# Two-block transformer kernel: S5 parameters in whole rows, x and the first weights in turns on one queue, loads moved from ACT's queue

## The chip, the cores and the metric

The kernel runs on one core of a Trainium2 chip. The metric is the device time of one execution in microseconds. The engines are TensorE (PE in the rows, PEld its weight loads), VectorE (DVE), ScalarE (ACT), GpSimd (POOL) and SyncE (SP); a q behind a name (ACTq) is that engine's instruction queue when it issues a DMA.

## The reference

256 tokens of width 2048 pass two layers of a first block and one layer of a second. Everything is float32. Cut to what matters:

```python
def layer_even(x, norm_g, w_in, w_out):          # first layer
    h = rmsnorm(x, norm_g)
    qa, ka, va, iq, ik, iw, qb, kb, vb, gate = split_cols(h @ w_in, SPLIT0)
    ... # attention A on the 64 best keys by an index score (iq, ik, iw); attention B with dilated windows
    return x + (concat(o_a, o_b) * silu(gate)) @ w_out

def s5_branch(u, z, a_re, a_im, log_dt, b_re, b_im, c_re, c_im, ...):   # in the second block
    dt = exp(log_dt)[:, None]
    mag = exp(a_re * dt)
    ab_re, ab_im = mag * cos(a_im * dt), mag * sin(a_im * dt)
    ...                                          # bb from ab, a and b; a scan over the tokens; c reads it out
```

The state-space parameters are small: a_re and a_im are 64 groups x 64 states, log_dt is one number a group, b_re and b_im are 64 x 64 x 16, c_re and c_im 64 x 16 x 64.

## The kernel before

A projection (`projW`, line 178) multiplies the normed input by a group of weight columns. float32 accuracy comes from three matmuls in a faster format: input and weights are each split into a high and a low part (`split`, line 145: ACT casts the high part at line 147, DVE subtracts to get the low part at lines 106 and 150), and high x high, high x low and low x high are summed in PSUM. Weights come in chunks of 256 rows (`weights`, line 157): one DMA on SP's queue for each run of columns at line 170 (six `raw` buffers), one cast, one subtraction (three buffers `wh` and `wl`), then 24 matmuls for four blocks of 128 columns. The chunk loads and splits stand at a raised priority. The code is traced in program order, and a scheduler puts each engine's instructions into an order by priority and by its own model of when each is ready; at run time an engine takes them in that order, its DMA issues among them, and waits for each.

`first_block` (line 613) starts the work. norm0's rows and the four pieces of x (256 tokens x 512 columns, 512 KB) are loaded from ACT's queue (lines 1507 and 626). `feed` (line 247) turns a piece on TensorE (line 127, eight transposes a piece) and splits it with norm0 as a factor (ACT line 118, DVE line 109). `squares`, `rstd` and `bcast` make the row norm's inverse: ACT squares, DVE sums, POOL takes the power (line 142), TensorE and ACT spread it over the partitions as `rb`. `params` (line 1517) then loads 15 rows of parameters from ACT's queue and turns them (lines 1507, 1511, 1513, 1541).

`even_layer` (line 387) projects in this order: a small group (ka, va, ik, iw: 336 columns, two DMAs a chunk), two groups of iq, three groups of qa. Each projection's PSUM (two buffers) is emptied at once by `rope` on DVE, scaled by rb; `ev_small` also turns iw and va on TensorE within its evacuation (lines 417 to 422). Behind the last qa group, at `K.hook()` (line 431), `s5_params` (line 670) is traced: nine loads from ACT's queue in the layout in which they are used (128 partitions = two groups x 64 states), so that a_re, a_im and log_dt are read 4 bytes at a time and b_re and b_im 64 bytes at a time (lines 683 to 688); then a chain of small operations on DVE and ACT in two scratch tiles (`yh`, `yl`), and sixteen transposes. Its results go to DRAM for later. After it come the attention `att()` (index scores, top-k on DVE, softmax), which runs beside the further projections, and the gate projections, which wait for it.

Of the kernel before, what the change touches and what calls it, by code (L numbers as in the profile page):

```python
# [16 lines left out]
D = 2048  # L17
S = 256
# [7 lines left out]
LAT = dict(bc=8.5, fd=10.0, fb=1.2, fh=0.8, z=0.3, sm=8.85, pt=1.42, st=6.0, ix=0.55, top=9.0, s5=11.0, inv=32.0, pr=1.3,  # L26
# [26 lines left out]
class Ker:  # L53
    def __init__(self, tc, a, es):
        self.tc, self.nc, self.a, self.es = tc, tc.nc, a, es
        self.n = 0
        self.after = lambda: None
# [62 lines left out]
    def mm(self, out, l, r, st=True, sp=True, **k):  # L120
        n = int(np.prod(r.shape[1:])) / 2.4
        self.clock += n if r.dtype == F32R else 4 * n * l.shape[0] / 128
        return self.nc.tensor.matmul(out, l, r, start=st, stop=sp, **k)  # L123
# [21 lines left out]
    def split(self, h, l, src, scale=None):  # L145
        if scale is None:
            self.nc.scalar.copy(h, src)  # L147
            self.tt(l, src, h.bitcast(F32), ALU.subtract)
        else:
            self.act(h, src, AF.Copy, scale=scale)  # L150
            self.stt(l, src, scale, h.bitcast(F32), ALU.mult, ALU.subtract)
# [5 lines left out]
    def weights(self, w, blocks, nk=KT, pool=None):  # L157
        runs, off = [], 0
        for c0, n in [r for b in blocks for r in (b if isinstance(b, list) else [b])]:
            if runs and runs[-1][0] + runs[-1][1] == c0:  # L160
                runs[-1][1] += n
            else:
                runs.append([c0, n, off])
            off += n
        KC = self.KC
        for kc in range(0, nk, KC):
          with self.tc.high_priority(offset=self.HP):
# [79 lines left out]
    def feed(self, xg, g, x, nw, ss=None):  # L247
        if ss is not None:
            self.squares(xg, g, ss)
        for k2 in range(0, 4, 2):  # L250
            pt = self.ps().rearrange("p (k s) -> p k s", k=2)
            for k in range(2):
                for t in range(2):
                    self.tr(pt[:, k, t * 128:t * 128 + 128], xg[:, t, (k2 + k) * 128:(k2 + k) * 128 + 128])
            for k in range(2):
                kk = 4 * g + k2 + k
                self.split(x[0][:, kk], x[1][:, kk], pt[:, k], nw if isinstance(nw, float) else nw[:, kk:kk + 1])

    def rstd(self, ss, name, n=D):
# [3 lines left out]
        r = self.t(self.pc, [128, 2], name)  # L263
# [4 lines left out]
    def bcast(self, r, name):  # L268
        o = self.t(self.pc, [128, S], name)
# [117 lines left out]
def even_layer(K, x, rbc, r, yo):  # L387
    nc, a = K.nc, K.a
    with ExitStack() as es:
# [19 lines left out]

        def ev_small(pt):  # L410
            K.tt(rp, rp, rbc.unsqueeze(1).to_broadcast([128, 4, S]), ALU.mult)
# [4 lines left out]
            K.tt(iwz[0:16], pt[64:80, 2], rbc[64:80], ALU.mult)  # L416
            p = K.ps()
# [12 lines left out]

        K.hook()
# [181 lines left out]
def first_block(K):  # L613
# [5 lines left out]
    with ExitStack() as es:  # L619
        K.pwk = K.pool("pre", 2, es)  # L620
        with K.tc.high_priority(offset=20000):
            n0 = load_params(K, [("norm0", a["norm0"].rearrange("(b p) -> b p", p=128), 16)], "pn", K.pwk)["norm0"]
            xgs = []
            for g in range(4):
                xg = K.t(K.pwk, [128, 2, 512], "xg", bufs=4)
                nc.scalar.dma_start(xg, xin[:, g * 512:g * 512 + 512].rearrange("(t p) c -> p t c", p=128))
                K.feed(xg, g, xt, n0)
                xgs.append(xg)
        for g in range(4):
            K.squares(xgs[g], g, ss[0])  # L630
        r0 = K.rstd(ss[0], "r0")
        rb0 = K.bcast(r0, "rb")
    prm = params(K)
# [3 lines left out]
    T = {}  # L637

# [31 lines left out]
def s5_params(K, ha, hb):  # L670
# [4 lines left out]
    dma = nc.scalar.dma_start  # L675
# [824 lines left out]
def load_params(K, rows, name, pool):  # L1500

    nc = K.nc
    t = K.t(pool, [128, 128], "prow")
    o = 0
    where = {}
    for key, ap, n in rows:
        nc.scalar.dma_start(t[o:o + n], ap)
        where[key] = (o, n)
        o += n
# [12 lines left out]
def params_(K, pool):  # L1522
# [5 lines left out]
                          ("kk", rw(a["rwkv_k_k_2"][0]), 8), ("ka", rw(a["rwkv_k_a_2"][0]), 8)], "pa", pool)  # L1528
# [3 lines left out]
                               ("gnw", a["gdn_norm_w_2"], 1)], "pb", pool))  # L1532
    prm.update(load_params(K, [("conv", a["gdn_conv_w_2"][0].rearrange("j (b p) -> (j b) p", p=128), 96)], "pv", pool))
# [247 lines left out]
```

## Time and profile before

| | us |
|---|---|
| median of 3 runs | 2217.39 (2214.86 to 2219.24) |
| the profiled execution, its own time | 2214.52 |
| its span, first to last instruction | 2212.7 |
| TensorE busy (matmul) | 2136.3, 97% |
| DVE busy | 1624.6, 73% |
| ACT busy | 1000.8, 45% |
| POOL busy | 37.8, 2% |

Busy shares are means over the whole span. The slices and windows of the rows below give them by stage. A matmul's duration overlaps the next one's, so the pace of matmuls is read from their count in a window; the granted clock beside it is 1.00 at 2.4 GHz and 0.50 at 1.2 GHz.

### The profile page before, as it was taken

Reading aid. Unit: us, or ns where it says so; the run is one execution under the profiler, and the core shown is the slowest. Engines: PE = TensorE matmul, PEld = TensorE weight load, DVE = VectorE, ACT = ScalarE, POOL = GpSimd, SP = SyncE. Lnnn points to the kernel's source line nnn. Section 1 sums busy time; section 2 is a strip of 40 time slices with the busy share of each in tenths; the row PEclk is TensorE's granted clock in tenths of the full one; section 3 lists DMA queues with packets and bytes.
Section 4 is the critical chain, followed back from the end, with each engine's and each line's share of the span. In section 5 each row is a group of like instructions: output and inputs, shape, how many; then the busy total and the mean of one; then the engine's idle time right before and its main releaser. Section 6 shows DMA issues by size and latency. Waiting matters only on the chain.

```text
span 2212.7 us, 38063 instructions
## 1 busy us (share of the span) xinstructions
PE 2136.3 (97%) x14946; PEld 1943.4 (88%) x14946; DVE 1624.6 (73%) x2845; ACT 1000.8 (45%) x1421; POOL 37.8 (2%) x85
## 2 busy tenths in 40 slices
PE   7499999999999999999999999999999999999998
PEld 7399999989989999989999989977778978979886
DVE  4387866657799866665578988989898857765665
ACT  4134454454345344454544433434346545534443
POOL 0010000000000000000000000000000000000000
PEclk9699999999999999999999999999999999999999
DMA  7355665676766665667677675676756667685774
GB/s 211 77 172 183 184 183 154 207 230 202 223 193 183 200 201 153 228 223 237 195 197 211 192 205 179 189 231 198 224 172 213 190 194 238 198 282 155 268 239 152
DMA packets 304249, 440.44 MB, mean 199 GB/s; under 512 B 73541, under 2 KB 135238, under 8 KB 303814
## 3 DMA queue, kind: packets, MB, share of 16 engines
q1 hardware_dynamic: 252048, 428.70, 62.7%
q10 hardware_dynamic: 52022, 9.31, 2.3%
q8 instruction: 117, 1.92, 0.4%
q14 instruction: 62, 0.51, 0.1%
HBM read 396.37 MB, written 41.57 MB: 198 GB/s over the span
## 4 chain that ended last, share of the span: by engine, by line
PE 81%; DVE 9%; DMA 4%; ACTq 2%; issue 2%; ACT 1%; POOL 0%; SPq 0%; DVEq 0%; POOLq 0%
PE pj L123 70%; PE ps L123 9%; DVE wl L106 3%; PE ps L127 2%; ACTq L687 1%; DMA raw<-in_w_in_dram 1%; DVE s5w L106 1%; DMA dim<-b 1%; DVE b L106 1%; ACTq L688 1%; ACT wh L147 1%; DMA e<-dim 1%; DMA s5r<-s5u 0%; POOL grs L142 0%; DVE G L106 0%
## 5 line engine op out<-in xcount | busy, mean ns | idle before, releaser
L147 ACT CAST wh<-raw 128x1024 fp32r<-128x1024 f32 (+5 forms) x680 | 685.0, 1009 | 950.9 <-PE pj L123 757.4
L106 DVE TENSOR_TENSOR wl<-raw,wh 128x1024 fp32r<-128x1024 f32 (+5 forms) x680 | 794.9, 1171 | 410.5 <-ACT wh L147 398.7
L123 PE MATMUL pj<-xh,wh 128*128 128x256 f32 (+1 forms) x2864 | 825.2, 288 | 13.9 <-ACT wh L147 13.0
L123 PE MATMUL pj<-xh,wl 128*128 128x256 f32 (+1 forms) x2864 | 816.1, 285 | 1.3 <-DVE wl L106 1.2
L123 PE MATMUL pj<-xl,wh 128*128 128x256 f32 (+1 forms) x2864 | 814.6, 284 | 0.3 <-DVE xl L109 0.3
L123 PEld LDWEIGHTS pj<-xh,wh 128*128 128x128 f32 (+1 forms) x2864 | 550.8, 192 | 26.7 <-ACT wh L147 13.4
L123 PEld LDWEIGHTS pj<-xh,wl 128*128 128x128 f32 (+1 forms) x2864 | 550.6, 192 | 6.0 <-issue 2.8
L123 PEld LDWEIGHTS pj<-xl,wh 128*128 128x128 f32 (+1 forms) x2864 | 551.0, 192 | 1.7 <-DVE xl L109 0.6
L123 PE MATMUL pj<-wh,xh 128*128 128x512 f32 (+2 forms) x736 | 283.4, 385 | 0.0
L123 PE MATMUL pj<-wh,xl 128*128 128x512 f32 (+2 forms) x736 | 279.1, 379 | 0.0
L123 PE MATMUL pj<-wl,xh 128*128 128x512 f32 (+2 forms) x736 | 278.8, 379 | 0.0
L123 PEld LDWEIGHTS pj<-wh,xh 128*128 128x128 f32 x736 | 138.8, 189 | 24.5 <-issue 3.0
L123 PEld LDWEIGHTS pj<-wl,xh 128*128 128x128 f32 x736 | 138.8, 189 | 23.6 <-issue 1.6
L123 PEld LDWEIGHTS pj<-wh,xl 128*128 128x128 f32 x736 | 138.6, 188 | 23.8 <-issue 1.2
L123 PE MATMUL pj<-wl,yh 128*128 128x512 f32 x256 | 99.9, 390 | 0.0
L123 PE MATMUL pj<-wh,yl 128*128 128x512 f32 x256 | 99.9, 390 | 0.0
L123 PE MATMUL pj<-wh,yh 128*128 128x512 f32 x256 | 99.7, 389 | 0.0
L123 PE MATMUL pj<-wh,E 128*128 128x512 f32 x192 | 76.7, 399 | 0.5 <-ACT wh L147 0.5
L123 PE MATMUL pj<-wl,E 128*128 128x512 f32 x192 | 75.0, 391 | 0.8 <-DVE wl L106 0.8
L123 PE MATMUL pj<-wh,G 128*128 128x512 f32 x192 | 75.2, 391 | 0.0
L106 DVE TENSOR_TENSOR raw<-yh,yl 128x256 f32<-128x256 f32 (+7 forms) x256 | 63.9, 287 | 3.5
L123 PEld LDWEIGHTS pj<-wh,yl 128*128 128x128 f32 x256 | 48.1, 188 | 9.9
(409 smaller groups left out, 2107.8 us busy)
## 6 DMA issues: line engine op xcount, KB each, us to landing
raw<-in_w_in_dram SPq DMA_DIRECT2D x416, 512.0 KB, 4.1
raw<-in_w_out_dram SPq DMA_DIRECT2D x96, 512.0 KB, 5.0
raw<-in_w_in_dram SPq DMA_DIRECT2D x96, 256.0 KB, 3.0
raw<-in_w_branch_dram SPq DMA_DIRECT2D x48, 512.0 KB, 5.3
raw<-in_w_in_dram SPq DMA_DIRECT2D x24, 344.0 KB, 3.1
s5t<-yh SPq DMA_DIRECT2D x16, 512.0 KB, 6.6
s5tb<-s5t SPq DMA_DIRECT2D x32, 256.0 KB, 4.6
raw<-in_w_in_dram SPq DMA_DIRECT2D x16, 384.0 KB, 4.0
```

What stands on the lines that cost most here:

```text
L106: return (eng or self.nc.vector).tensor_tensor(out=out, in0=a, in1=b, op=op)
L123: return self.nc.tensor.matmul(out, l, r, start=st, stop=sp, **k)
L127: return self.nc.tensor.transpose(out, a, self.ident)
L147: self.nc.scalar.copy(h, src)
L687: dma(br, a["s5_b_re_2"][0].rearrange("(i j) p c -> (j p) i c", j=2))
L688: dma(bi, a["s5_b_im_2"][0].rearrange("(i j) p c -> (j p) i c", j=2))
```

## The change

- The a and b parameters of S5 are loaded with groups on the partitions, in whole rows (32 rows of two groups each). log_dt is copied along its rows by POOL. One transpose (of 96 rows) and sixteen (of 64) on TensorE turn them into the former layout; they are ordered behind the last matmul traced before the hook (`issue_after`). All loads and stores of `s5_params` go from ACT's queue to POOL's.
- The other parameter rows (`params`) are loaded from POOL's queue, norm0's from SP's.
- The x pieces are loaded from SP's queue, into a tile that the S5 scratch takes over later. A callback in `weights` (`ahead`) puts x piece g ahead of weight chunk 4g of the first projection, and `issue_after` pins loads and splits to the order x0, w0, w2, x1, w4, w6, x2 and so on. A piece's transposes may start behind the chunk before last; its squares stand between two chunks' splits.
- The first projection is now the first group of iq (four blocks, 512 columns), the small group comes second, and the turns of iw and va become a step of their own (`turn_small`), due 12 us after the small group.
- The warm-up activation goes to the front of ACT, eight extra matmuls on the identity to the front of TensorE and eight on the first x piece behind its transposes; no one reads their results.

The diff's core:

```diff
-        warm = self.t(self.pc, [128, 1], "warm")
-        self.act(warm, self.mhalf[:, 0:1], AF.Tanh)
+        with self.tc.high_priority(offset=40000):
+            warm = self.t(self.pc, [128, 1], "warm")
+            self.act(warm, self.mhalf[:, 0:1], AF.Tanh)
+            self.dummies(self.ident, 8)
+
+
+    def dummies(self, m, n):
+        p = self.t(self.pm[1], [128, 512], "ps1")
+        for _ in range(n):
+            self.nc.tensor.matmul(p[:, 0:128], self.ident, m, start=True, stop=True)
...
+    def linked(self):
+        es = ExitStack()
+        for i in self.order:
+            es.enter_context(self.tc.issue_after(i))
+        return es
...
+          self.ahead(kc)
+          with self.tc.high_priority(offset=self.HP), self.linked():
             raw = self.t(self.pw, [128, KC, off], "raw", bufs=6)
             for c0, n, o in runs:
-                self.nc.sync.dma_start(
+                d = self.nc.sync.dma_start(
                     raw[:, :, o:o + n],
                     w[kc * 128:(kc + KC) * 128, c0:c0 + n].rearrange("(k p) c -> p k c", p=128))
             h, l = (self.t(pool or self.pw, [128, KC, off], tag, F32R, bufs=8 if pool else 3) for tag in ("wh", "wl"))
-            self.split(h, l, raw)
+            i = self.split(h, l, raw)
+          if self.order:
+              self.order = [d.ins] + i
           yield kc, h, l
...
+        def ev_iq(pt, g):
+            if g == 0:
+                K.tt(rp, rp, rbc.unsqueeze(1).to_broadcast([128, 4, S]), ALU.mult)
+            K.rope(iq[:, 4 * g:4 * g + 4], pt, 4, 64, C2, T2)
+
...
+        def turn_small():
+            yield LAT["small"]
             p = K.ps()
             for t in range(2):
                 K.mm(p[:, t * 16:t * 16 + 16], iwz[:, t * 128:t * 128 + 128], K.ident[:, 0:16])
                 K.tr(p[:, 256 + t * 128:384 + t * 128], vaT[:, t * 128:t * 128 + 128])
             nc.vector.tensor_copy(iw, p[:, 0:32].rearrange("p (t c) -> p t c", t=2))
             nc.scalar.copy(va, p[:, 256:512].rearrange("p (t c) -> p t c", t=2))
+        qi = lambda g: K.projW(w, [(1536 + g * 512 + b * 128, 128) for b in range(4)], x, lambda pt: ev_iq(pt, g))
+        qi(0)
         K.projW(w, [(1280, 128), (1408, 128), (2560, 80)], x, ev_small)
-        for g in range(2):
-            K.projW(w, [(1536 + g * 512 + b * 128, 128) for b in range(4)], x,
-                    lambda pt, g=g: K.rope(iq[:, 4 * g:4 * g + 4], pt, 4, 64, C2, T2))
+        turned = K.flow(turn_small(), (0, 0, 0, 1))
+        qi(1)
...
-    with ExitStack() as es:
-        K.pwk = K.pool("pre", 2, es)
-        with K.tc.high_priority(offset=20000):
-            n0 = load_params(K, [("norm0", a["norm0"].rearrange("(b p) -> b p", p=128), 16)], "pn", K.pwk)["norm0"]
-            xgs = []
-            for g in range(4):
-                xg = K.t(K.pwk, [128, 2, 512], "xg", bufs=4)
-                nc.scalar.dma_start(xg, xin[:, g * 512:g * 512 + 512].rearrange("(t p) c -> p t c", p=128))
-                K.feed(xg, g, xt, n0)
-                xgs.append(xg)
-        for g in range(4):
-            K.squares(xgs[g], g, ss[0])
-        r0 = K.rstd(ss[0], "r0")
-        rb0 = K.bcast(r0, "rb")
-    prm = params(K)
     ey = ExitStack()
     py = K.pool("y0", 1, ey)
     spare = lambda p: [K.t(p, [128, 4096], t) for t in ("yh", "yl")]
     T = {}
+    xall, scr = spare(py)
+    xgs = [xall[:, 1024 * g:1024 * g + 1024].rearrange("p (t c) -> p t c", t=2) for g in range(4)]
+    with K.tc.high_priority(offset=20000):
+        n0 = load_params(K, [("norm0", a["norm0"].rearrange("(b p) -> b p", p=128), 16)], "pn", None, nc.sync.dma_start,
+                         scr[:, 0:128], K.order)["norm0"]
+    r0, rb0 = K.t(K.pc, [128, 2], "r0"), K.t(K.pc, [128, S], "rb")
+
+    prm, behind = {}, K.order[-1]
+
+
+
+    def ahead(kc):
+        nonlocal behind
+        g = kc // 4
+        if kc % 4 == 0:
+            with K.tc.high_priority(offset=20000), K.linked(), K.tc.issue_after(behind):
+                d = nc.sync.dma_start(xgs[g], xin[:, g * 512:g * 512 + 512].rearrange("(t p) c -> p t c", p=128))
+                i = K.feed(xgs[g], g, xt, n0)
+                if g == 0:
+                    K.dummies(xgs[0][:, 0, 0:128], 8)
+            K.order = [d.ins] + i
+            return
+        behind = K.last
+        with K.linked():
+            for t in range(2):
+                K.act(scr[:, 512 + 512 * t:1024 + 512 * t], xgs[g][:, t], AF.Square, accum_out=ss[0][:, t, g:g + 1])
+        if g == 3:
+            K.ahead, K.order = lambda kc: None, []
+            K.rstd(ss[0], "r0", r=r0)
+            K.bcast(r0, "rb", rb0)
+            prm.update(params(K))
+    K.ahead = ahead
...
-    dma = nc.scalar.dma_start
+    dma = nc.gpsimd.dma_start
     big = [ha[:, 512 * i:512 * i + 512] for i in range(8)]
     v32 = lambda x: x.rearrange("p (i c) -> p i c", c=16)
     br, bi, t2, bbr, bbi = (v32(x) for x in big[0:5])
@@ -680,12 +729,29 @@
     small = [big[7][:, 32 * i:32 * i + 32] for i in range(16)]
     take = lambda: small.pop(0)
     ar, ai, ld = take(), take(), take()
-    dma(ar, a["s5_a_re_2"][0].rearrange("(i j) p -> (j p) i", j=2))
-    dma(ai, a["s5_a_im_2"][0].rearrange("(i j) p -> (j p) i", j=2))
-    for j in range(2):
-        dma(ld[64 * j:64 * j + 64], a["s5_log_dt_2"][0].rearrange("(i j) -> j i", j=2)[j].partition_broadcast(64))
-    dma(br, a["s5_b_re_2"][0].rearrange("(i j) p c -> (j p) i c", j=2))
-    dma(bi, a["s5_b_im_2"][0].rearrange("(i j) p c -> (j p) i c", j=2))
+    Z, lj = big[3][0:96, 0:128], big[4][64:96, 0:2]
+    jp = lambda name: a[name][0].rearrange("(i j) p -> i (j p)", j=2)
+    dma(Z[0:32], jp("s5_a_re_2"))
+    dma(Z[32:64], jp("s5_a_im_2"))
+    dma(lj, a["s5_log_dt_2"][0].rearrange("(i j) -> i j", j=2))
+    B = hb[0:64, 2048:4096]
+    for i, name in enumerate(("s5_b_re_2", "s5_b_im_2")):
+        dma(B[32 * i:32 * i + 32], a[name][0].rearrange("(i j) p c -> i (j p c)", j=2))
+    nc.gpsimd.tensor_copy(Z[64:96].rearrange("i (j p) -> i j p", j=2), lj.unsqueeze(2).to_broadcast([32, 2, 64]))
+    behind = K.last
+    p = K.ps()
+    with K.tc.issue_after(behind):
+        nc.tensor.transpose(p[:, 0:96], Z, K.ident[0:96, 0:96])
+    nc.vector.tensor_copy(big[7][:, 0:96], p[:, 0:96])
+    Bc = B.rearrange("i (m c) -> i m c", c=16)
+    for c in (0, 8):
+        p = K.ps()
+        with K.tc.issue_after(behind):
+            for u in range(8):
+                nc.tensor.transpose(p[:, 64 * u:64 * u + 64], Bc[:, :, c + u], K.ident[0:64, 0:64])
+        pv = p.rearrange("p (c r i) -> p c r i", c=8, r=2)
+        for r, o in enumerate((br, bi)):
+            nc.scalar.copy(o[:, :, c:c + 8].rearrange("p i c -> p c i"), pv[:, :, r])
...
```

`load_params` takes the issuing queue as an argument: SP's for norm0, POOL's in the three calls of `params`. `rstd` and `bcast` can take a ready tile, and `mm` keeps the last matmul as `K.last`.

## Rows read from the trace of the kernel before

**Rows 1.** The page's 40 slices of 55 us: busy tenths of TensorE

```profile
PE   7499999999999999999999999999999999999998
```

**Rows 2.** Windows: us, busy (count) of each engine, granted clock, DMA share, GB/s

```profile
0.00:12.50 12.50, 4.78 (x19) 3.61 (x19) 1.49 (x4) 3.38 (x6) 1.18 (x9) 1.00 0.87 282
12.50:36.00 23.50, 23.50 (x181) 23.50 (x181) 16.77 (x31) 17.68 (x41) 0.72 (x1) 1.00 0.86 260
44.00:98.30 54.30, 16.54 (x99) 15.28 (x98) 8.24 (x20) 4.42 (x7) 0.00 (x0) 0.64 0.31 45
```

**Rows 3.** Chain that ended last, in order of time: start us, us, what

```profile
53.58 22.49 ACTq L687
77.21 16.31 ACTq L688
```

**Rows 4.** Timeline of ACT: start us, us, instruction, count, idle before it

```profile
52.56 23.51 ACTq L687 DMA_DIRECT2D yh<-in_s_b_re_dram  x1
76.17 1.04 ACT L147 CAST wh<-raw 128x1024 fp32r<-128x1024 f32 x1 [22.59 <-issue]
76.19 17.33 ACTq L688 DMA_DIRECT2D yh<-in_s_b_im_dram  x1
95.97 1.04 ACT L147 CAST wh<-raw 128x1024 fp32r<-128x1024 f32 x1 [18.76 <-issue]
```

**Rows 5.** Windows of TensorE alone, behind the hole

```profile
97.00:103.20 6.20, 5.67 (x25) 0.50 0.91 243
```

**Rows 6.** Windows of line 123, all projection matmuls: PE, PEld, clock, DMA

```profile
11.50:34.20 22.70, 20.79 (x150) 19.39 (x151) 1.00 0.88 268
34.20:103.18 68.98, 30.93 (x196) 29.47 (x195) 0.68 0.41 82
103.18:183.90 80.72, 80.72 (x673) 80.59 (x672) 1.00 0.59 173
```

**Rows 7.** Lines 1507 and 687: longest parameter issue; landing of one b load

```profile
L1507 ACTq DMA_DIRECT2D prow<-in_rwkv_mu_dram x1: 632/632/632, 28.4 to 28.4; - x1
...
DMA to landing us min/median/max: 41.9/41.9/41.9
```

**Rows 8.** Groups by form, 0 to 45 us: busy us, mean ns, idle

```profile
L118 ACT ACTIVATE xh<-ps,pnc 128x256 fp32r<-128x256 f32 x16 | 6.9, 476 | 0.9 <-PE ps L127 0.9
L106 DVE TENSOR_TENSOR wl<-raw,wh 128x1024 fp32r<-128x1024 f32 x5 | 6.1, 1224 | 3.8 <-ACT wh L147 3.8
L147 ACT CAST wh<-raw 128x1024 fp32r<-128x1024 f32 x5 | 5.3, 1050 | 7.2 <-PE pj L123 7.2
L118 ACT ACTIVATE junk<-xg 128x512 f32<-128x512 f32 x8 | 5.0, 625 | 0.0
```

**Rows 9.** Timeline of TensorE: the sixteen S5 transposes

```profile
183.82 1.91 PE L127 MATMUL ps<-ident,yl 128*128 128x128 f32 x16
```

**Rows 10.** Windows of DVE on S5's scratch tiles, yh and then yl

```profile
98.30:150.00 51.70, 7.89 (x29) 0.95 0.66 192
...
98.30:150.00 51.70, 4.53 (x19) 0.95 0.66 192
```

**Rows 11.** Windows behind the hook, all engines

```profile
215.00:230.00 15.00, 15.00 (x118) 14.48 (x118) 14.78 (x41) 5.42 (x9) 0.00 (x0) 1.00 0.57 173
230.00:250.00 20.00, 19.27 (x158) 18.66 (x157) 19.29 (x49) 10.40 (x14) 0.00 (x0) 1.00 0.77 222
300.00:330.00 30.00, 30.00 (x201) 29.86 (x201) 16.05 (x30) 15.64 (x26) 0.00 (x0) 1.00 0.71 202
```

**Rows 12.** Window of 2 us in the start: DMA engines' share and GB/s last

```profile
10.00:12.00 2.00, 1.11 (x5) 0.58 (x3) 0.81 (x2) 1.99 (x4) 0.00 (x0) 1.00 1.11 373
```

**Rows 13.** Line 626's issues of x, then ACT's and TensorE's timelines

```profile
L626 ACTq DMA_DIRECT2D xg<-in_x_dram x4: 374/426/527, 1.2 to 8.7; - x4
...
9.11 1.28 ACT L147 ACT_TABLE_LOAD   x1 [9.11 <-DMA xg<-in_x_dram]
...
11.58 0.58 PE L123 MATMUL pj<-xh,wh 128*128 128x256 f32 x1 [0.89 <-ACT xh L118]
```

More of the change, by code (lines that the diff above doesn't have):

```diff
@@ L22 @@
 MARK = -3.0e38
-LAT = dict(bc=8.5, fd=10.0, fb=1.2, fh=0.8, z=0.3, sm=8.85, pt=1.42, st=6.0, ix=0.55, top=9.0, s5=11.0, inv=32.0, pr=1.3,
+LAT = dict(small=12.0, bc=8.5, fd=10.0, fb=1.2, fh=0.8, z=0.3, sm=8.85, pt=1.42, st=6.0, ix=0.55, top=9.0, s5=11.0, inv=32.0, pr=1.3,
            prz=1.6, feat=15.0, prod=2.2, c1=1.25, c3=1.3, gn=11.0, sc=6.5, conv=22.5, ln=4.1, rw=2.3, rb=9.0, gp=1.0,
@@ L56, in __init__ @@
         self.n = 0
-        self.after = lambda: None
+        self.after = self.hook = lambda: None
+        self.ahead, self.order = lambda kc: None, []
         self.pc = self.pool("const", 1)
@@ L122, in mm @@
         self.clock += n if r.dtype == F32R else 4 * n * l.shape[0] / 128
-        return self.nc.tensor.matmul(out, l, r, start=st, stop=sp, **k)
+        i = self.nc.tensor.matmul(out, l, r, start=st, stop=sp, **k)
+        self.last = i.ins
+        return i
     def tr(self, out, a):
@@ L146, in split @@
         if scale is None:
-            self.nc.scalar.copy(h, src)
-            self.tt(l, src, h.bitcast(F32), ALU.subtract)
-        else:
-            self.act(h, src, AF.Copy, scale=scale)
-            self.stt(l, src, scale, h.bitcast(F32), ALU.mult, ALU.subtract)
+            i = self.nc.scalar.copy(h, src)
+            j = self.tt(l, src, h.bitcast(F32), ALU.subtract)
+        else:
+            i = self.act(h, src, AF.Copy, scale=scale)
+            j = self.stt(l, src, scale, h.bitcast(F32), ALU.mult, ALU.subtract)
+        return [i.ins, j.ins]
+    def linked(self):
[3 more added lines that the diff above has]
+        return es
     KC = 2
@@ L166, in weights @@
         for kc in range(0, nk, KC):
-          with self.tc.high_priority(offset=self.HP):
+          self.ahead(kc)
+          with self.tc.high_priority(offset=self.HP), self.linked():
             raw = self.t(self.pw, [128, KC, off], "raw", bufs=6)
             for c0, n, o in runs:
-                self.nc.sync.dma_start(
+                d = self.nc.sync.dma_start(
                     raw[:, :, o:o + n],
@@ L256, in feed, with rstd @@
                 kk = 4 * g + k2 + k
-                self.split(x[0][:, kk], x[1][:, kk], pt[:, k], nw if isinstance(nw, float) else nw[:, kk:kk + 1])
-    def rstd(self, ss, name, n=D):
+                i = self.split(x[0][:, kk], x[1][:, kk], pt[:, k], nw if isinstance(nw, float) else nw[:, kk:kk + 1])
+        return i
+    def rstd(self, ss, name, n=D, r=None):
         s1 = self.t(self.pc, [128, 2], name + "s")
@@ L262, in rstd, with bcast @@
         self.ts(s1, s1, 1.0 / n, EPS, ALU.mult, ALU.add)
-        r = self.t(self.pc, [128, 2], name)
+        r = self.t(self.pc, [128, 2], name) if r is None else r
         self.rsqrt(r, s1, 2)
         return r
-    def bcast(self, r, name):
-        o = self.t(self.pc, [128, S], name)
+    def bcast(self, r, name, o=None):
+        o = self.t(self.pc, [128, S], name) if o is None else o
         def steps():
@@ L429, in even_layer @@
                     lambda pt, g=g, nb=nb: K.rope(y[:, g:g + nb], pt[:, 0:nb], nb, 128, C1, T1))
+        K.drain(turned)
         K.hook()
@@ L1497, in branch, with load_params @@
         self.sums = True
-def load_params(K, rows, name, pool):
+def load_params(K, rows, name, pool, dma, t=None, order=None):
     nc = K.nc
-    t = K.t(pool, [128, 128], "prow")
+    t = K.t(pool, [128, 128], "prow") if t is None else t
     o = 0
@@ L1506, in load_params @@
     for key, ap, n in rows:
-        nc.scalar.dma_start(t[o:o + n], ap)
+        d = dma(t[o:o + n], ap)
+        if order is not None:
+            order.append(d.ins)
         where[key] = (o, n)
@@ L1531, in params_ @@
                                ("s5d", rw(a["s5_d_2"][0]), 8), ("glubh", rw(a["s5_glu_b_2"][0]), 8),
-                               ("gnw", a["gdn_norm_w_2"], 1)], "pb", pool))
-    prm.update(load_params(K, [("conv", a["gdn_conv_w_2"][0].rearrange("j (b p) -> (j b) p", p=128), 96)], "pv", pool))
+                               ("gnw", a["gdn_norm_w_2"], 1)], "pb", pool, nc.gpsimd.dma_start))
+    prm.update(load_params(K, [("conv", a["gdn_conv_w_2"][0].rearrange("j (b p) -> (j b) p", p=128), 96)], "pv", pool, nc.gpsimd.dma_start))
     for h in ("w0h", "a0h", "glubh"):
```

3 lines of the change are left out of this document (1 added, 2 removed).

## Prediction

> **What bounds the kernel now.** I read the page's forty slices first: TensorE is nine tenths busy everywhere except in the first slice, the second, where it falls to 0.4, and the very last [rows 1]. So the change is judged in the first 110 us alone. The table of stages puts a size on it: TensorE works 16.54 of the 54.30 us from 44 to 98.3, a hole of 37.8 us, and 4.78 of the first 12.5 us [rows 2]. Outside these two stretches it idles 31 us in all (2212.7 - 2136.3 - 37.8 - 7.7), none of it near the change.
>
> The chain of waits says what ended last in the hole: not a computation and not a transfer, but ACT's own issuing of two loads, lines 687 and 688, 22.5 and 16.3 us of path [rows 3]. ACT's timeline shows what that does. The instructions on a queue start in order, so the casts of line 147, which make the weights' high halves, stand behind the issues and come one at a time, after 22.59 and 18.76 us in which ACT waited for nothing that the profile shows [rows 4]. TensorE needs a cast per 24 matmuls and runs dry. So the hole is sequencer time, spent on loads cut into runs of 64 bytes (16 floats), or of 4 bytes for a_re, a_im and log_dt.
>
> **The hole, in matmuls.** Idle time alone understates it, because TensorE comes back at half clock: 25 matmuls in 6.20 us at a granted 0.50, which is 1.2 of 2.4 GHz [rows 5], against 673 in 80.72 us at 1.00, or 0.120 us each [rows 6]. Therefore I count work. From 34.20 to 103.18 stand 196 records [rows 6], eight of them small ones of the broadcast and of iwz; 188 x 0.120 = 22.6 us, and I allow 1.7 us for these eight, two row turns of the parameters and two turns of vaT. Needed 24.3, spent 69.0: **the hole costs 44.7 us.** Without it the last matmul ahead of the hook, at 183.9 now, would stand at 139.2.
>
> **Part by part.**
>
> *Loads in whole rows, off ACT's queue (-44.7).* The a and b loads become 32 rows of 512 bytes and of 8 KB, log_dt 32 runs of 8 bytes: over a hundred times fewer pieces for b. They, the parameter rows and the S5 stores go to POOL's queue, where they delay no cast even if slow. What is late next is the cast waiting for a free wh buffer, that is TensorE itself, as after 110 us. All -44.7 counts.
>
> *POOL's queue.* The trace of before has no DMA issued there. Nearest are ACT's issues of the same parameter rows, 0.63 us the longest [rows 7]; upper end, the 23.5 us that line 687 took in its worst layout [rows 4]. For rows I take 1 us. Queued behind these loads on POOL is r0's power (line 142), on which rb and so the first evacuation hang, and on TensorE and DVE the turns and copies of the parameters (lines 1511, 1513), not pinned behind anything. The first is covered only until the small projection ends: the rope of the first projection reads its PSUM for about 12 us (six operations of 1.22 [rows 8], interleaved with low halves) out of 16.6, so rb may be 3 us late for nothing and costs one for one after that. I take +1 us, ends 0 and 5; a gain is excluded, since TensorE didn't wait for either before the hole.
>
> *Turning on TensorE (+1.8).* One transpose of 96 rows and 16 of 64 rows. The nearest row is 16 transposes of 128 in 1.91 us [rows 9]; half the columns bounds them at 1, and full price at 2; five copies out of PSUM on ACT and DVE go beside other work. They are held behind the last matmul before the hook, some 100 us after the loads can be issued, hence wait for nothing.
>
> *S5's vector work moves past the hook (+1.5).* Before, 12.4 us of it (7.89 and 4.53 on the two scratch tiles) ran at 98 to 150 [rows 10], in DVE's gaps. Now it can't begin ahead of the turns. From 215 on DVE is 14.78 of 15.00, then 19.29 of 20.00 us busy with the top-k, and TensorE idles 0.73 us in that last stretch; after 250 there is room, 16.05 of 30 [rows 11]. Weights and evacuations go first by priority, the attention flow only has to be ready for the gate projections far behind. So most of it delays work that waits anyway. Ends 0 and 6 (half of 12.4, if half meets the full stretch); I take 1.5, near the 0.73 now seen.
>
> *The start (-3.6).* Now the four x pieces on ACT's queue share the DMA engines with up to 12 weight loads; the engines are saturated at 373 GB/s [rows 12], 1.4 us for 512 KB. The last x load is issued at 8.7, ACT's first computation stands behind it (table load at 9.11), and the first projection matmul starts at 11.58 [rows 13]. 150 matmuls, with the 32 turns of x between them, take until 34.2 [rows 6]. After: order x0, w0, w2, x1, w4, w6 and so on. With data moving from 2 us, x0 is there at about 4.5 and each further piece 1.4 later, the twelfth at 20, ahead of use. By row means [rows 8]: 8 turns at half clock, 2.0, with ACT behind them, 4 x 0.48 for xh and 1.05 for w0: first matmul at 8.5; DVE 1.2 more for wl; 24 matmuls until 12.5, during which the clock comes up. From there each pair of chunks costs 8 turns (0.9), 48 matmuls (5.8) and 0.4 for a cast that comes late (ACT needs 2 x 1.05 + 4 x 0.48 + 2 x 0.63 = 5.3 of those 7 us): 19.6, 26.7, 33.8, and 36.7 with the last chunk. Small projection 16.6, then 672 matmuls 80.6 and 1.7 odds: the hook at 135.6 against 139.2. Ends: -6.5 if ACT never makes it wait and the clock rises at once, 0 if the single queue brings x0 no sooner than before. The 16 dummies fall into TensorE's wait for x0 and for ACT; the warm Tanh takes the 1.28 us table load out of the way; both lie inside the figures above. The later turn of iwz and vaT takes a wait out of the hole and is in the 44.7.
>
> **Sum.** -44.7 - 3.6 + 1.8 + 1.5 + 1 = -44.0. The profiled execution took 2214.5 (span 2212.7 and 1.8 around), so 2170.5 on that scale; the median of the runs, 2217.4, lies 2.9 above the profiled one: **2173 us**. Best ends: -44.7 - 6.5 + 1 = -50.2, 2167; worst -44.7 + 2 + 6 + 5 = -31.7, 2186. The three runs spread by 4.4 us, and everything later is put in order anew by the scheduler, for which I give the low end 4 us more.
>
> **The rivals.** *DVE becomes the bound behind the hook.* For it: 14.78 of 15.00 us [rows 11]. Against it: TensorE lost 0.73 us there, and room follows at 250. If all 12.4 us land on the path, 11 more than taken: 2184.
>
> *POOL makes transfers only while DVE rests.* The trace of before can't show it. DVE is busy 16.77 of 23.50 us from 12.5 to 36 [rows 2], so a load of 1 us would take 3.5, fifteen parameter loads 52, and r0's power would come near 54 instead of 33. The evacuation of the first projection would start some 15 us later than is covered, and the third projection waits for its PSUM: 2173 - 1 + 15 = 2187. The Trainium skill (SBUF — State Buffer, "SBUF: two separate sides") speaks against the change in this way: descriptors of DMAs issued from GpSimd go through a port pair that a VectorE operation in a two-port mode locks, so they starve while it runs. DVE's long operations here move 1024 columns in 1.22 us [rows 8], hardly a fast mode, so I give it a tenth.
>
> *Slower.* The turns of b are pinned in TensorE's order, so if POOL's loads land after the hook, TensorE stands still until they do. The loads can be issued from about 32 (their tile is x's), the hook is at 136. On ACT the two b loads alone took from 52.56 to 93.5 to issue, 41 us [rows 4], and the first of them 41.9 from issue to landing [rows 7]. POOL would have to need over 104 us for its set before anything is lost, and over 148 before the kernel is slower; at four times ACT's 41, 164, the turns come at 196 instead of 136: 2173 + 60 = 2233.
>
> *It doesn't do what it says.* If ACT's casts were held by saturated DMA engines and not by ACT's own issuing, the hole would stay and the start bring little: 2215. Against it: the engines are nearly idle in the hole, DMA share 0.31 [rows 2].
>
> **How the numbers follow.** Forecast 0.75; DVE 0.10; POOL behind DVE 0.10; unchanged 0.02; slower 0.03. Predicted is the forecast's 2173; the range, 2163 to 2187, reaches to the two middle rivals and leaves the last two out. A measurement of this kernel tells about 0.2% (4.4 us) from no change: the first three are faster by more than that, 0.95; unchanged (2215) is within it, 0.02; slower 0.03.
>
> **What would show it.** Right: no issue of DMAs on ACT's queue in the first 150 us; no TensorE gap over 5 us after 10; first projection matmul at 8 to 9; the first projection's end near 37 and the last matmul ahead of the turns near 136; the turns directly behind it. Wrong: a stretch at half clock between 20 and 250; TensorE waiting for a DMA of POOL or for DVE's rope at about 53; gaps of several us from 136 to 200 (DVE). If the hook is at 136 and the time above 2180, the loss lies behind the hook.

## The result, and the profile after

The changed kernel took 2186.05 us (median of four runs, 2182.97 to 2187.11), the kernel before beside it 2217.1: a ratio of 0.9858, 95% interval 0.9841 to 0.9875, or 31 us. The forecast was 2173, the range 2163 to 2187. The time lies inside the range, at its upper end, and 13 us of the forecast gain are missing.

The table of stages of the kernel after: start and end in us, length, TensorE's busy time (count), granted clock, DMA share, GB/s.

```profile
0.00:12.50 12.50, 8.94 (x54) 0.98 0.85 283
12.50:36.00 23.50, 22.05 (x169) 0.94 0.64 219
36.00:54.00 18.00, 18.00 (x156) 1.00 0.94 256
54.00:139.00 85.00, 85.00 (x713) 1.00 0.60 178
139.00:165.00 26.00, 24.65 (x205) 1.00 0.51 151
165.00:190.00 25.00, 24.47 (x167) 1.00 0.64 209
190.00:215.00 25.00, 10.03 (x62) 0.69 0.48 143
215.00:250.00 35.00, 35.00 (x284) 0.97 0.40 111
```

The hole of [rows 2] is gone: from 36 to 139 TensorE has no idle slice. A new hole stands at 190 to 215, 15 us of idle time, and the clock falls with it to 0.69 on average.

TensorE's timeline of the kernel after, at the places that the prediction named (start us, us, engine, line, operation, what stood before it and who ended that):

```profile
9.63 0.39 PE L132 MATMUL pj<-xh,wh 128*128 128x256 f32 x1 [0.74 <-ACT wh L158]
10.89 0.39 PE L132 MATMUL pj<-xh,wl 128*128 128x256 f32 x1 [0.76 <-DVE wl L115]
14.90 1.27 PE L138 MATMUL ps<-ident,yh 128*128 128x128 f32 x8
139.07 0.25 PE L744 MATMUL ps<-ident,yh 96*128 96x96 f32 x1
139.25 2.00 PE L751 MATMUL ps<-ident,yl 64*128 64x64 f32 x16
141.18 0.39 PE L132 MATMUL pj<-xh,wh 128*128 128x256 f32 x1
205.68 0.97 PE L138 MATMUL ps<-ident,zb 128*128 128x128 f32 x2 [10.53 <-DVE zb L123]
210.88 1.11 PE L138 MATMUL ps<-ident,zb 128*128 128x128 f32 x4 [4.23 <-DVE zb L123]
213.87 0.56 PE L132 MATMUL pj<-xh,wh 128*128 128x256 f32 x1
398.68 0.40 PE L132 MATMUL pj<-wh,yh 128*128 128x512 f32 x1
```

The hook, told by S5's first turn, stands at 139.07 (183.9 before, [rows 6]), the other turns directly behind it. Then, at 205.68 and 210.88, TensorE stands 10.53 and 4.23 us for softmax scores that VectorE has not finished.

**A landmark.** The last row is the first matmul of the first block's output projection. In the kernel before it is this:

```profile
422.91 0.40 PE L123 MATMUL pj<-wh,yh 128*128 128x512 f32 x1
```

So the change is worth 24.2 us up to here. Behind it both kernels do the same work: 1789.8 us to the span's end before, 1786.6 after. In the eleven experiments below that stretch took 1786.8 to 1794.7. I therefore judge each edit by the landmark, and give its time beside it; a time carries up to 8 us of what happens later. A landmark comes from one profiled execution: two profiles of the changed kernel put it 1.2 us apart, two of the kernel with its own tile (below) 1.0.

### The profile page after: what moved, and what is told of

The parts are those of the page before. It is cut to its first block, busy times and chain, and to the rows that moved or that the text cites. A ratio compares the mean times of both kernels' runs of the same rounds, so it can differ in the third digit from the quotient of the medians.

```text
span 2185.3 us, 38189 instructions
## 1 busy us (share of the span) xinstructions
PE 2135.0 (98%) x14995; PEld 1944.7 (89%) x14995; DVE 1627.7 (74%) x2846; ACT 1004.6 (46%) x1425; POOL 48.8 (2%) x113
## 5 line engine op out<-in xcount | busy, mean ns | idle before, releaser
L132 PE MATMUL pj<-xh,wh 128*128 128x256 f32 (+2 forms) x2864 | 822.1, 287 | 0.7 <-ACT wh L158 0.7
L132 PE MATMUL pj<-xh,wl 128*128 128x256 f32 (+2 forms) x2864 | 814.2, 284 | 3.9 <-DVE wl L115 3.9
L132 PE MATMUL pj<-xl,wh 128*128 128x256 f32 (+2 forms) x2864 | 812.1, 284 | 0.0
L132 PEld LDWEIGHTS pj<-xh,wh 128*128 128x128 f32 (+2 forms) x2864 | 548.6, 192 | 11.9 <-issue 8.6
L132 PEld LDWEIGHTS pj<-xh,wl 128*128 128x128 f32 (+2 forms) x2864 | 548.6, 192 | 8.4 <-DVE wl L115 5.5
L132 PEld LDWEIGHTS pj<-xl,wh 128*128 128x128 f32 (+2 forms) x2864 | 548.8, 192 | 1.0 <-issue 0.3
L132 PEld LDWEIGHTS pj<-wh,yh 128*128 128x128 f32 x256 | 48.1, 188 | 9.9
```

What stands on the lines that cost most here:

```text
L132: i = self.nc.tensor.matmul(out, l, r, start=st, stop=sp, **k)
```

## The experiments

**Theory** at the outset: S5's 12 us of vector work, now behind the hook, keep VectorE from the index scores and the top-k, so that TensorE waits for softmax scores (the prediction's first rival). **Rival theories:** S5's step holds a buffer that the projections need; POOL's queue; the start.

*S5's step earlier.*

```diff
         qi(1)
+        K.hook()
...
         K.drain(turned)
-        K.hook()
```

> The changed kernel with S5's step called after the third projection (528 matmuls in, about 81 us) instead of after the sixth (1008 matmuls, 139 us); its turns are pinned there. Nothing else. Theory (the 12.4 us of S5's vector work, put behind the hook, pushes index scores and top-k back until TensorE waits for them): the stands of 10.53 and 4.23 us at 205.7 and 210.9 go, and the half clock behind them; from the last matmul ahead of the old hook's place to the third pair of softmax turns, 110.7 us in the changed kernel and 90.1 in the one before, it takes 91 to 94. Time 2186 - 16 = 2170, 2166 to 2175. Rival (the loss is POOL's queue or comes from other places): 2182 to 2188. Rival (the vector work at 81 to 110 us makes casts or evacuations late there): TensorE idles 5 us or more ahead of 139, time 2176 to 2185.

Measured: 2179.08 us, ratio 0.9849 (0.9828 to 0.987), over the 2166 to 2175 of the theory; landmark at 387.33, 11.4 us earlier than in the changed kernel. The stands (idle times of TensorE) at 205 and 210 went, but a new one came. VectorE's and TensorE's timelines of this kernel:

```profile
133.41 1.23 DVE L115 TENSOR_TENSOR ropeA<-pj,ropec 128x1024 f32<-128x1024 f32 x1 [0.88 <-DMA s5b<-ropeA]
150.25 2.46 DVE L115 TENSOR_TENSOR ropeB<-pj,ropec 64x1024 f32<-64x1024 f32 x2
152.76 0.58 PE L132 MATMUL pj<-xh,wh 128*128 128x256 f32 x1 [6.86 <-DVE ropeB L115]
```

The evacuation of a projection waits at 133.41 for a DMA that stores S5's b table from ropeA, and gets to ropeB 17 us later; TensorE stands 6.86 us for that ropeB. Ahead of that wait there was vector time to spare: VectorE was busy 5.42 of the 13.40 us from 120 to 133.4. Once the evacuation is late, index scores and top-k stand in VectorE's order between its two halves and fill it, 18.23 of the 19.40 us until 152.8. Line 824 stores the table from two scratch tiles, ropeA and ropeB, which each projection's evacuation (the emptying of its PSUM) uses too. In the changed kernel SP's issues of these stores and VectorE's evacuation of the first projection behind the hook show the same; the next experiment was set up from these rows, along with this one:

```profile
176.03 7.23 SPq L824 DMA_DIRECT2D s5b<-ropeA  x7
183.31 0.96 SPq L824 DMA_DIRECT2D s5b<-ropeB  x2
197.88 3.46 SPq L824 DMA_DIRECT2D s5b<-ropeB  x6
```

```profile
192.04 1.22 DVE L115 TENSOR_TENSOR ropeA<-pj,ropec 128x1024 f32<-128x1024 f32 x1
211.12 2.46 DVE L115 TENSOR_TENSOR ropeB<-pj,ropec 64x1024 f32<-64x1024 f32 x2
```

ropeB's last store is issued at 201.3 and lands 3.1 us later (the median of these eight), and VectorE's order has the two ropeB products behind the whole top-k, at 211.12. They end at 213.58; at 213.87 TensorE starts its next projection.

*The b table in a tile of its own.*

```diff
-        h, l = (K.t(K.pwk, [128, 4, S], tag, F32R) for tag in ("ropeA", "ropeB"))
+        h, l = (hb[:, o:o + 1024].bitcast(F32R).rearrange("p (v m) -> p v m", v=4) for o in (2048, 3072))
```

> The changed kernel, but the two halves of S5's b table are written to a free part of yl instead of the scratch tiles ropeA and ropeB, which the evacuations of the projections use too. S5's vector work stays behind the hook, as much of it as before. Theory 1 (the amount of vector work behind the hook is the loss): index scores and top-k are as late as now, TensorE still stands 10 us or more between 190 and 215, time 2181 to 2188. Theory 2 (what is lost is the shared scratch: the evacuation of the first projection behind the hook gets ropeB only at 211.1, behind the stores of the b table and the whole top-k, so that TensorE has no PSUM for the third projection): the evacuation comes ahead of the top-k, no stand over 3 us from 139 to 260, time 2186 - 15 = 2171, 2168 to 2176.

Measured: 2174.73 us, ratio 0.9824 (0.9808 to 0.984); landmark at 384.42, 14.3 us earlier than in the changed kernel. Of this 1.4 stand before the hook already (137.69), 12.9 behind it. Its hook and landmark, its stages (as above) and the evacuation:

```profile
137.69 0.25 PE L744 MATMUL ps<-ident,yh 96*128 96x96 f32 x1
384.42 0.40 PE L132 MATMUL pj<-wh,yh 128*128 128x512 f32 x1
```

```profile
139.00:165.00 26.00, 24.66 (x205) 1.00 0.45 138
165.00:190.00 25.00, 24.58 (x188) 1.00 0.75 243
190.00:215.00 25.00, 24.46 (x166) 1.00 0.42 111
```

```profile
165.13 1.23 DVE L115 TENSOR_TENSOR ropeA<-pj,ropec 128x1024 f32<-128x1024 f32 x1 [1.04 <-PE pj L132]
166.99 2.46 DVE L115 TENSOR_TENSOR ropeB<-pj,ropec 64x1024 f32<-64x1024 f32 x2
```

The evacuation comes at 165 instead of 192 to 214, as soon as its matmuls end, though S5's vector work stands where it stood. The hole at 190 is gone. Theory 2 holds. The scheduler's order behind the hook is another one too: the first softmax turns stand at 218.16 instead of 205.68, with projection matmuls ahead of them. That belongs to what was measured.

*Both kernels side by side.* The two again on one chip:

> The changed kernel once more, unchanged, beside the next two on one chip, since earlier runs stood beside kernels before of 2210 to 2217 us. Theory and rivals alike: 0.984 to 0.988 of the kernel before, the output projection's first matmul at 397 to 401 us, TensorE's stands of about 10 and 4 us at 205 and 211.

> The changed kernel with the b table in a free part of yl, once more, beside the changed kernel itself. Theory (the shared scratch is the loss): the output projection's first matmul 13 to 15 us earlier than in the changed kernel, at 383 to 387, and the time 11 to 15 us shorter. Rival (the gain seen before was in part the chip): 5 to 9 us shorter.

Measured: changed kernel 2186.92 us, ratio 0.9882 (0.9865 to 0.9898), landmark 397.44, stands of 10.52 and 4.22; own tile 2179.01, 0.9844 (0.9826 to 0.9861), landmark 385.37. The landmark gains 12.1, a little under what I expected and inside its bounds (383 to 387); the time gains 7.9, short of the 11 to 15 and inside the 5 to 9 that the rival asked for. So at the landmark the tile is worth 12 to 14 us, in time 8 to 11. The rest of the span took 5.7 us more in the second (1794.7 against 1789.0). About 2 us of that come from one place: from 400 to 600 us behind the landmark TensorE is busy 197.73 and 197.75 of 200 us in the two profiles with the own tile, 200.00 and 199.56 in the two without. For the rest I have no cause. The landmarks, of the changed kernel and of the own tile:

```profile
397.44 0.40 PE L132 MATMUL pj<-wh,yh 128*128 128x512 f32 x1
```

```profile
385.37 0.40 PE L132 MATMUL pj<-wh,yh 128*128 128x512 f32 x1
```

*Twice the vector work.* On top of the own tile:

```diff
     K.tt(cim, cim, den, ALU.mult)
+    for _ in range(18):
+        K.tt(hb[:, 2048:2560], big[0], big[1], ALU.mult)
```

> Own scratch as before, and S5's chain of vector work doubled: 18 more VectorE products of 128 x 512, about 12 us, whose results nothing uses, in the chain ahead of the b table's products. It doses the suspect that my rival named. Theory (the amount of vector work behind the hook costs little as long as nothing the projections need is held): the output projection's first matmul 0 to 4 us later than with own scratch alone, 384 to 389, time 2174 to 2179. Rival (VectorE is the bound there): 9 to 12 us later, 393 to 397, time 2183 to 2187.

Measured: 2179.90 us, ratio 0.9842 (0.9823 to 0.9862), landmark 389.66. Some 12 us of further vector work cost 4.3 us at the landmark and 0.9 in time. TensorE's one new wait of over 1 us is for POOL's copies at the end of S5's chain, and the granted clock is 0.74 from 190 to 200. That wait and the landmark:

```profile
190.08 1.11 PE L138 MATMUL ps<-ident,yl 128*128 128x128 f32 x4 [4.00 <-POOL yl L814]
389.66 0.40 PE L132 MATMUL pj<-wh,yh 128*128 128x512 f32 x1
```

So vector work there is not free (I expected 0 to 4), but it cost about a third of its length, most of it in one wait at the end of the chain, though VectorE was busy 19.46 of the 20.00 us from 170 to 190. My rival, which asked for 9 to 12, falls.

*Early step and own tile together.*

> Both edits together: S5's step after the third projection, and its b table written to a free part of yl instead of ropeA and ropeB. With the changed kernel (2186), the early step alone (2179.1) and the own scratch alone (2174.7) it makes a square. Theory (what is lost is the shared scratch alone, early or late): no stand over 3 us from 100 to 260, and about what the own scratch gives alone, 2171 to 2175. Rival (the amount of vector work behind the hook costs something of its own): the early step brings a further 5 to 8 us, 2166 to 2170.

Measured: 2177.71 us, ratio 0.9856 (0.9839 to 0.9873), beside a kernel before of 2210.0; landmark 387.0. With the own tile the early step brings nothing (387.0 against 384.4 and 385.4), and with the early step the own tile brings 0.3 (387.0 against 387.33). So the two gains, 11.4 and 14.3, don't add up: they remove the same loss. The time was over the 2171 to 2175 of my theory. The square is not quite clean: this kernel has a stand of its own, 1.91 us for POOL's copies at 121.81, with a granted clock of 0.83 from 120 to 130.

*The old start.* x in four pieces on ACT's queue and the small projection first, no dummies; S5's loads and turns, and POOL's queue, stay as changed.

```diff
-            self.dummies(self.ident, 8)
...
-        qi(0)
         K.projW(w, [(1280, 128), (1408, 128), (2560, 80)], x, ev_small)
-        turned = K.flow(turn_small(), (0, 0, 0, 1))
-        qi(1)
+        for g in range(2):
+            K.projW(w, [(1536 + g * 512 + b * 128, 128) for b in range(4)], x,
...
+                nc.scalar.dma_start(xg, xin[:, g * 512:g * 512 + 512].rearrange("(t p) c -> p t c", p=128))
+                K.feed(xg, g, xt, n0)
...
-    K.ahead = ahead
```

> The changed kernel with the start of the kernel before: x in four pieces on ACT's queue ahead of everything, weights beside them, the small projection first, no dummy matmuls. S5's rows, turns and POOL's queue stay as changed. By my sum the start brought 3.6 us: hook at 142.7 and 2189.7. By the trace of the changed kernel (hook at 139.07, where the sum without the start gave 139.2) it brought nothing: hook at 138 to 140, time 2183 to 2188. Behind the hook the same stands of about 15 us in either case.

Measured: 2191.58 us, ratio 0.9898 (0.9882 to 0.9914); hook at 143.09, landmark 403.0. By the hook that seemed to bear my 3.6 out. But TensorE's timeline shows the place:

```profile
34.95 0.27 PE L1551 MATMUL ps<-ident,prow 88*128 88x88 f32 x1 [2.82 <-DMA prow<-in_rwkv_lnx_b_dram]
```

TensorE stood 2.82 us for parameter rows, which POOL issued only from 27.2 on, about 0.5 us each, and came back at half clock (granted 0.50 from 37 to 38). So the next run gave the parameter rows back to ACT's queue as well:

```diff
 def load_params(K, rows, name, pool, dma, t=None, order=None):
...
-                          ("kk", rw(a["rwkv_k_k_2"][0]), 8), ("ka", rw(a["rwkv_k_a_2"][0]), 8)], "pa", pool, nc.gpsimd.dma_start)
+                          ("kk", rw(a["rwkv_k_k_2"][0]), 8), ("ka", rw(a["rwkv_k_a_2"][0]), 8)], "pa", pool, nc.scalar.dma_start)
```

> The changed kernel with the whole start of the kernel before: as in the run with the old start, and the parameter rows issued from ACT's queue as they were. S5's rows and their turns stay on POOL's queue. It parts the 4.0 us that the old start cost at the hook (143.09 against 139.07). Theory (they were the wait for parameter rows that POOL's queue brought late, 2.82 us and half clock behind it; x and weights by turns bring nothing): hook at 138.5 to 140, the output projection's first matmul at 397 to 400. Rival (turns of x and weights bring the 3.6 us of my sum): hook at 142 to 143.5, the output projection at 402 to 404.

Measured: 2192.3 us, ratio 0.9888 (0.9867 to 0.991); landmark 400.78, and the hook:

```profile
139.10 0.25 PE L716 MATMUL ps<-ident,yh 96*128 96x96 f32 x1
```

139.10 with the whole old start, 139.07 with the new one in the first profile of the changed kernel. That profile is the latest of five with the new start, which put the hook at 137.69 to 139.07 (below). So up to the hook x and weights by turns bring 0 to 1.4 us, less than the 3.6 of the sum. The landmark is 2.1 later than in the first profile of the changed kernel and 3.3 later than in the second; this kernel waited 2.30 for POOL's copies at 166, the changed one 1.35. In time it is 5 to 6 us behind the changed kernel (2192.3 against 2186.05 and 2186.92), while the intervals of the three ratios overlap. What of that belongs to the start is not shown. By time alone the two runs of the old start can't be told apart.

*No dummies.*

```diff
-            self.dummies(self.ident, 8)
...
-                if g == 0:
-                    K.dummies(xgs[0][:, 0, 0:128], 8)
```

> The changed kernel without the 16 dummy matmuls ahead of the first piece of x. With them TensorE shows a granted clock of 1.00 up to 11.9 us and the 8 turns of x take 1.10; in the old start the turns took 1.97. Theory (the dummies buy the clock of the first turns and of some 12 matmuls): turns 1.97, first projection matmul at 10.3 to 10.6 instead of 9.6, the clock full from 15 as now, so the hook at 140 to 141 and the time 2187 to 2188. Rival (the clock falls at 11.9 anyway, and what comes later is set by loads and casts): hook at 139.1, 2185 to 2187.

Measured: 2188.98 us, ratio 0.9906 (0.9889 to 0.9922); first matmul at 10.46, hook at 139.44, landmark 401.1. At the hook the dummies are worth 0.4 to 1.8 us against the five profiles that have them, and the time lies over both forecasts, so theory and rival stay undecided. The dummies don't always have their effect: in the run of the changed kernel beside the own tile, the eight turns of x at 5.99 took 1.97 us, as here without dummies, and not the 1.09 of the first profile (the granted clock reads 1.00 there in all three).

*All loads back on ACT's queue, rows whole.*

```diff
-    dma = nc.gpsimd.dma_start
+    dma = nc.scalar.dma_start
```

and the same in the three calls of load_params.

> The changed kernel with the same whole rows, but every load of S5 and of the parameter rows issued from ACT's queue again. It tells whether POOL's queue is needed once the rows are whole. Theory (what held the casts was the issue of short runs): 5 loads of S5's rows and 2 of c issue in 0.3 to 1 us each (0.39 for a_re before), some 5 us in ACT's gaps; the 15 parameter rows, 0.26 to 0.63 each before, stand ahead of ACT's first work at 6.7 us and may make x late by 0 to 2 us: 2184 to 2190, no TensorE stand over 3 us from 37 to 139. Rival (any load on ACT's queue holds the casts): stands of 10 us or more there, 2195 to 2215.

Measured: 2195.85 us, ratio 0.9932 (0.9916 to 0.9949); landmark 409.1, 10.4 later. ACT's and TensorE's timelines:

```profile
9.01 1.28 ACT L127 ACT_TABLE_LOAD   x1 [9.01 <-DMA prow<-in_rwkv_r_k_dram]
45.79 0.32 ACTq L739 DMA_DIRECT2D yl<-in_s_b_re_dram  x1
48.26 0.32 ACTq L739 DMA_DIRECT2D yl<-in_s_b_im_dram  x1
```

```profile
15.68 0.58 PE L132 MATMUL pj<-xh,wh 128*128 128x256 f32 x1 [7.26 <-ACT wh L158]
```

S5's b rows now issue in 0.32 us each on ACT's queue, where the old layout took 23.51 and 17.33 [rows 4], and TensorE doesn't stand from 50 to 139: for S5 the queue doesn't matter once rows are whole. What costs is the fifteen parameter rows ahead of ACT's first computation. It starts at 9.01 instead of 1.20, and the first matmul comes 6.05 us later, of the 10.4 at the landmark. I had allowed 0 to 2 for that; the time lies in my rival's range, but its stands between 37 and 139 did not come.

*The old layout on POOL's queue.* a, b and log_dt as before, the turns left out.

```diff
-    dma(Z[0:32], jp("s5_a_re_2"))
+    dma(ar, a["s5_a_re_2"][0].rearrange("(i j) p -> (j p) i", j=2))
...
-        dma(B[32 * i:32 * i + 32], a[name][0].rearrange("(i j) p c -> i (j p c)", j=2))
+    dma(br, a["s5_b_re_2"][0].rearrange("(i j) p c -> (j p) i c", j=2))
```

> The changed kernel with a, b and log_dt loaded in the old layout (runs of 4 and of 64 bytes), but from POOL's queue; the 17 turns on TensorE and their copies are left out, for nothing is left to turn. It tells whether the queue or the whole rows closed the hole. If POOL needs about as long as ACT did (41 us for b), everything is there by about 100 us, S5's vector work runs ahead of the hook, no stand behind it: 2186 - 18 = 2168, 2165 to 2175. If POOL needs four times as long (the prediction's slower case), the work comes behind the hook again, without being waited for by turns: 2180 to 2190; if r0's power is queued behind these loads on POOL, TensorE waits for the first evacuation, up to 40 us: 2200 to 2230.

Measured: 2209.39 us, ratio 0.9977 (0.9968 to 0.9986), landmark 420.7: nearly nothing is left of the gain. POOL's, ACT's and TensorE's timelines, and the DMA issues between 30 and 100 us (KB each, median us to landing):

```profile
44.93 1.71 POOL L736 DMA_DIRECT2D yh<-in_s_b_re_dram  x1 [2.24 <-issue]
85.02 0.23 ACT L127 ACTIVATE yh<-yh 128x32 f32<-128x32 f32 x1 [42.41 <-DMA yh<-in_s_log_dt_dram]
85.98 0.58 PE L132 MATMUL pj<-xh,wh 128*128 128x256 f32 x1 [31.28 <-ACT wh L158]
```

```profile
yh<-in_s_b_re_dram POOLq DMA_DIRECT2D x1, 256.0 KB, 41.9
yh<-in_s_log_dt_dram POOLq DMA_DIRECT2D x2, 8.0 KB, 34.0
```

POOL issues the load in 1.71 us, and it still takes 41.9 to land, as on ACT's queue [rows 7]. ACT's exponential of log_dt stands in ACT's order ahead of the casts and waits 42.41 us for its load; TensorE runs dry again. In whole rows the same 256 KB landed in 5.6 us in the changed kernel. The time lies in the range of my third case, but r0's power, which that case made late, ran at 39.78. The queue without the rows moves the wait from the issue to the landing; the rows are what closes the hole.

## Why the prediction was right or wrong

- **The hole (-44.7): right.** With the old start the hook went from 183.8 to 139.10. That this is 44.7 to the tenth is luck, since one and the same start put the hook up to 1.4 us apart (next item). Counting needed matmuls, not idle time, was the right measure. The rival "it doesn't do what it says" was wrong about this change. Half of the change does leave the hole: on POOL's queue in the old layout ACT waits for a load to land, with the DMA engines' share at 0.82 from 55 to 86.
- **The start (-3.6): too large; 0 to 1.4 at the hook.** One profile of the old start has 139.10. Five of the new start have 139.07, 138.41, 137.69, 138.67 and 138.37 (changed kernel twice, own tile twice, doubled vector work). In these five and in the one without dummies the hook stands 123.9 to 124.2 us behind the second turns of x (14.90 in the first), so what sets them apart happens in the first 15 us. The step that failed is the one that set the new start against an assumed 139.2 and not against work done: at 34.2 the old start had made 150 records of projection matmuls [rows 6], the new one 146 (150 in the first profile with the own tile). x0's turns start at 6.01, where the sum had x0 there at 4.5. The first matmul does come earlier, 9.63 (forecast 8.5, before 11.58), but the first 24 matmuls last until 14.90 instead of 12.5, with a wait for wl, and in this profile a stretch at half clock (granted 0.50 from 12 to 15) that the second one, 14.47, does not have. Each round of eight turns and 48 matmuls then takes 7.7 us on average (14.90 to 22.69, and to 30.24; 7.6 in the other four) instead of 7.1. The first projection's end, worked out as 36.7, came near 40.6 (170 records until 38.0, 22 more at 0.12). The sum has a slip too: the small projection's 144 matmuls are 17.3 us at its own 0.120, not 16.6, which by itself makes the forecast gain 2.9.
- **POOL's queue (+1, 0 to 5): 0 here.** The parameter rows are requested from 1.70 us on and no TensorE wait names them; r0's power stood at 37.90 between S5's loads and rb came at 41.42, in time. Under the old start the same queue cost 4.0, so the range was fair.
- **Turns (+1.8): right.** 139.07 to 141.18 is 2.1.
- **S5's vector work (+1.5, 0 to 6): here lies the main loss.** Hook to landmark was 239.1 us (183.8 to 422.9) and became 259.6. Less the turns, 18.4. With the own tile it is 246.7 in both runs of it, so 12.9 of the 18.4 go with the shared scratch, and with the new order that came with its end; 5.5 are left for vector work, inside my ends. What failed is the sentence that weights and evacuations go first by priority: an evacuation whose scratch is held doesn't. I had asked only whose engine time the moved step takes, and not which tiles it holds; the sum has no term for it. Before, S5's stores from ropeA and ropeB were issued from 3 us behind the hook on, and the evacuation of the first projection behind it came at 223.69, 40 us behind. Now the vector chain runs first, the stores start 29 us behind the hook (168.53), and fall on the evacuation that the projections wait for.
- **The rivals.** "DVE becomes the bound" had nearly the right time, 2184, and the wrong mechanism: twice the vector work cost a third of its length, and the own tile ended the stands with all of it in place. That the time lies inside the range is therefore luck: the range reached up to 2187 for two rivals, and neither came. "POOL makes transfers only while DVE rests" did not come: S5's loads were issued between 36.9 and 39.6 in 0.5 us each and landed in 2.8 to 6.4, with VectorE busy 8.50 of the 11.00 us from 36 to 47. The Trainium skill (SBUF — State Buffer, "SBUF: two separate sides") lets VectorE hold up such descriptors in its two-port modes; no run here shows it. "Slower" stayed far: whole rows landed some 90 us ahead of the turns.
- **The signs.** No issue of S5's or the parameters' loads on ACT's queue except one of 0.43 us at 0.74; no gap over 5 us from 10 to 190; the hook 3 us later than the 136 named. The sign for the other case, the hook in place and the time above 2180, held but for these 3 us, and pointed to where the loss was. One sign of being wrong came as well, a stretch at half clock between 20 and 250: granted 0.50 from 205 to 215.

Missing on the profile's scale: the profiled execution took 2187.1 (span and 1.8) where the sum gave 2170.5, or 16.6. Of these 12.9 are the scratch, 3.6 the start (in this profile, the latest of the five), 4.0 more vector work than taken (5.5 - 1.5), 0.3 the turns; -1 POOL's queue and about -3.2 the later stages, which in this execution were shorter. What stays open: why the later stages differ by up to 8 us between executions of kernels alike there, and how the stands would have been with TensorE's order changed alone, since the softmax turns stand ahead of the projection in it and the own tile changed both.

The version to keep is the changed kernel with the b table in its own tile: 0.9824 and 0.9844 of the kernel before in its two comparisons.

## What to carry to other kernels

When a step is moved, list the tiles, PSUM banks and scratch it holds and until when, not only the time of its engines: here 12 us of further vector work cost 4 at the landmark, and two borrowed tiles 12 to 14 (8 to 11 in time). A new start is worth what it gains at a fixed count of matmuls, not at the first of them, and one profile of each is not enough where the same start varies by 1.4 us. And a load in short runs costs twice, at the queue that issues it and until it lands: moving it to another queue only changes who waits.

## What the runs showed of the hardware

- The load of b in runs of 64 bytes took ACT's queue 23.51 us to issue [rows 4] and POOL 1.71, and landed after 41.9 us from either. In rows of 8 KB ACT issued it in 0.32 and POOL in 0.49, and from POOL's queue the two b loads landed in 4.2 to 6.4 (two profiles). The Trainium skill (DMA: Bandwidth & Descriptors, "Specifications") asks for 512 bytes and more for the full rate, and the trace agrees as far as it goes: 64 bytes are far slower than 8 KB, and no load of this size was tried near 512. How unequal the two queues are in issuing short runs I had not expected.
- One and the same start runs differently from execution to execution: with the same dummies, the eight turns of x took 1.09 us in two of the five profiles named under the start and 1.97 in three. The hook lay between 137.69 and 139.07, with 1.09 at both of these ends.
- Sixteen turns of 64 rows took 2.00 us, no less than the sixteen of 128 rows before, 1.91 [rows 9].
